# RWKV-7 layer of a hybrid decoder step: products, merges and gate of the late work in the dense products' PSUM banks

## The chip, the cores and the metric

The kernel runs on one core of one Trainium2 chip. The metric is the device time of one execution in microseconds; the kernel before takes 1889.89 us (median of three runs, 1886.84 to 1902.13). TensorE (PE) multiplies matrices into PSUM; VectorE (DVE), ScalarE (ACT) and GpSimd (POOL) read the results from there and work on them; SyncE (SP) issues DMA transfers, as ACT does for the weights.

## The reference

One inference step of a two-layer decoder in float32. Layer 0 mixes with a gated DeltaNet, layer 1 with RWKV-7; a causal ConvFFN follows each. 512 prompt tokens behind 16 meta tokens run as one sequence, 32 sample tokens (8 sequences of 4) from given states. Only the RWKV-7 mixer bears on the change:

```
def rwkv_step(S, xs):
    r_t, w_t, k_t, v_t, kk_t, a_t = xs
    sa = jnp.einsum('bhvk,bhk->bhv', S, kk_t)
    S = (S * w_t[:, :, None, :] - sa[..., None] * (kk_t * a_t)[:, :, None, :]
         + v_t[..., None] * k_t[:, :, None, :])
    y = jnp.einsum('bhvk,bhk->bhv', S, r_t)
    return S, y
...
    r = xr @ wr
    k = xk @ wk
    v = xv @ wv
...
    gate = jax.nn.sigmoid(xg @ g1) @ g2
...
    S, y = lax.scan(rwkv_step, S0.astype(F32), (tm(rh), tm(dh), tm(kh), tm(vh), tm(kk), tm(ah)))
...
    y = ((y - mu) * lax.rsqrt(var + GN_EPS)).reshape(B, L, D) * ln_w.astype(F32) + ln_b.astype(F32)
    bonus = jnp.sum(rh * kh * r_k.astype(F32), axis=-1, keepdims=True) * vh
    y = y + bonus.reshape(B, L, D)
    out = (y * gate.astype(F32)).astype(h.dtype) @ wo
```

The model width is 1024, with 16 heads of 64.

## The kernel before

All 560 tokens (32 sample, 16 meta, 512 prompt) lie in the free dimension, the 1024 channels as 8 blocks of 128 partitions. A dense product splits weights and input into a high and a low part and runs three matmuls for one (`dense_g`, L99, matmuls L114).

The function `rwkv` (from L1100) replaces the scan over tokens by chunks: chunk 0 of 48 tokens (16 of them meta), then eight of 64. The 16 heads go in two halves, G = 0 (the first heads) and G = 1 (the second heads). For a half and a chunk:

- `products` (L1412): 8 matmuls (L1420) into two PSUM banks give the chunk's 64 x 64 products of keys, receptances and decays; DVE masks them into SBUF (L1427, for chunk 0 L1424), POOL scales one block (L1433).
- `early` and `to_inverse` bring the triangular part of all chunks to DRAM; `inverse` (L1469) inverts the 32 x 32 triangles of chunks 1 to 8 at once on DVE (`tri_inplace`, L1071 and L1072), sends them to DRAM (UI) and loads them back into the products' tiles A (L1483, 16 DMAs on SP). `inverse0` does this for chunk 0.
- `merge` (L1505) makes 64 x 64 inverses out of 32 x 32 ones, for two chunks at a time (q = 0 to 3): a transpose on DVE (L1510), PE L1514, ACT L1515, PE L1519, ACT. Each merge starts the next.
- `rec` (L1639) is the serial recurrence of a half. After chunk 0 (L1665 to L1683), a chunk is a chain: PE L1695 and L1699, ACT L1700, PE L1704, DVE L1636, PE L1713, DVE L1715, then the next chunk; PE L1722 and DVE L1723 give its output. The second half's recurrence starts after the first's.
- `outnorm` (L1737) normalises two chunks' outputs (PE L1762), `samples` (L1779) runs the sample sequences (L1822 to L1845), `ktokens` and `vtokens` (L1540, L1562, L1584) rearrange keys and values, `gates` (L1596) computes the gate: 16 groups of four matmuls (L1618, L1619; 8 blocks, two halves of the tokens), each read by ACT (L1620) and DVE (L1621).

**PSUM.** It has eight banks. The pool `pd` (set up for the whole program) has two tiles of two banks, used by all dense products. The pool `pr` (L1108) has four single banks, handed out by `bank` (L487): recurrence, products, merges, norms, samples and gate share them in turn.

**Order.** The class `Weave` (L407) interleaves two kinds of generators with a modelled clock. `chains` are tried first, each with a time from which it may go on, as long as no more than two banks of `pr` are counted as held (`step`). Where none may, the next piece of the `slots` is issued. The slots of this layer stand in a row: dense k, r and v (8 blocks each), the products of the second heads (`products2`), the gate, and the output product of the first heads (osA, `out_half`). The output product of the second heads (osB) follows when all is done. A scheduler of the framework then sets the final order of each engine by its own estimates. Each engine takes its instructions in that order.

```
                if c[1] <= self.now and len(self.banks) <= 2:
```

```
        W.slots += [[None, products2()], [lambda: all(ktdone) and len(zdone) == KD and prod_done[1], gates()],
                    [lambda: normed[0] == 6 and bool(gated), out_half()]]
```

Of the kernel before, what the change touches and what calls it, by code (L numbers as in the profile page):

```python
# [8 lines left out]
F32 = mybir.dt.float32  # L9
# [8 lines left out]
P = 128  # L18
# [6 lines left out]
KD = 8  # L25
# [461 lines left out]
def bank_of(pg):  # L487
    def bank(shape):
        t = pg.tile([P, 512], F32, tag="pg", name="pg")
        n = int(np.prod(shape))  # L490
        v = t[:, :n]
        if len(shape) == 2:
            v = v.rearrange("p (a b) -> p a b", a=shape[0])
        elif len(shape) == 3:
            v = v.rearrange("p (a b c) -> p a b c", a=shape[0], b=shape[1])
        return v
    return bank


# [600 lines left out]
def rwkv(E, xp, norm, x_dram, sink):  # L1100


    nc, I, O = E.nc, E.I, E.O
    st = ExitStack()
    with st:
# [260 lines left out]
        def by_block(G, q):  # L1366
# [7 lines left out]
            nc.sync.dma_start(out=Dd[G], in_=t)  # L1374


        stA = ExitStack()
# [27 lines left out]
        def all_products(G):  # L1405
            for c in range(1, 9):
                A[G][c] = B["lo" if c < 5 else "hi"][G][:, (c - 1) % 4]
            for c in range(9):
                yield from products(G, c)
            prod_done[G] = True  # L1410

        def products(G, c):  # L1412

            o, n = col64(c)

            pa = [bank([4, 2, 64]) for hh in range(2)]
            for u in range(4):
# [48 lines left out]

        prod_done, merged = [False, False], [set(), set()]

        def inverse(G):  # L1469
            X, tmp = B["X"], B["tmp"]  # L1470
            nc.sync.dma_start(out=X, in_=LI[G].rearrange("j c h i t -> (j c h) i t"))
            for j in range(2):
                nc.sync.dma_start(out=D[64 * j:64 * j + 64], in_=Dd[G, 8:72, 32 * j:32 * j + 32])
            nc.vector.tensor_tensor(X, X, D.unsqueeze(1).to_broadcast([P, 32, 32]), op=ALU.mult)
            for _ in tri_inplace(E, X, tmp, P, 32):
                yield 0, E.d3, 0
            nc.sync.dma_start(out=UI[G].rearrange("j c h i t -> (j c h) i t"), in_=X)
            yield 0, E.invlag2, 0
            while not prod_done[G]:
                yield None  # L1480
            for c in range(8):
                for j in range(2):
                    nc.sync.dma_start(out=A[G][c + 1][64 + 32 * j:96 + 32 * j, :, 1, 32 * j:32 * j + 32],  # L1483
                                      in_=UI[G, j, c].rearrange("h i t -> i h t"))
            yield 0, 3.0, 0
            W.chain(merge(G, 0), first=True)

        def inverse0(G):
# [8 lines left out]
            yield 0, 8.0, 0  # L1497
            while not prod_done[G]:
                yield None
# [5 lines left out]
        def merge(G, q):  # L1505
# [5 lines left out]
            yield 0, 0.8, 0  # L1511
            py = bank([16, 32])
            for h in range(16):
                nc.tensor.matmul(py[r2, h, :], lhsT=Ac[r1, h, 1, 32:64], rhs=TY[r1, h, :], start=True, stop=True)  # L1514
            nc.scalar.activation(TY[r2], py[r2], AF.Copy)  # L1515
            yield 1.0, 1.0, 1
            pu = bank([16, 32])
            for h in range(16):
# [3 lines left out]
            merged[G].update((2 * q + 1, 2 * q + 2))  # L1522
            if q < 3:
                W.chain(merge(G, q + 1), first=True)

# [24 lines left out]
        v = H  # L1550
# [45 lines left out]
        def gates():  # L1596
# [4 lines left out]
            for b in range(2):  # L1601
# [13 lines left out]
                for m in range(KD):  # L1615
                    ps = bank([280])
                    for w, x in ((hi, gh), (hi, gl), (lo, gh)):
# [259 lines left out]
        def products2():  # L1877
            second_room()
            for w in all_products(1):
                yield w[0]  # L1880

        def seconds():
            for i, (r, f) in enumerate(((dn, ev_a), (up, ev_w))):
# [5 lines left out]
        W.slots += [[None, slot(ev_v(m))] for m in range(KD)]  # L1889
        W.slots += [[None, products2()], [lambda: all(ktdone) and len(zdone) == KD and prod_done[1], gates()],  # L1890
                    [lambda: normed[0] == 6 and bool(gated), out_half()]]
# [239 lines left out]
```

## Time and profile before

| | |
|---|---|
| median of three runs | 1889.89 us (1886.84 to 1902.13) |
| the profiled execution's own time | 1896.1 us |
| its span, first to last instruction | 1894.3 us |
| mean granted clock of TensorE | 0.951 |
| PE, DVE, ACT, POOL busy | 95%, 61%, 38%, 19% of the span |

The profile is of one execution. "Busy" of PE counts matmuls in flight, at whatever clock was granted to it, so that a stretch can be fully busy and still slow. In rows of the timeline the number in front is the start within the span, then the length; what stands in brackets is the idle time of the engine just before, and what ended it. The change touches the RWKV layer between about 1129 us, where the order of PE's instructions first differs, and 1429 us, where osB starts.

### The profile page before, as it was taken

The page shows a single profiled execution, that of the slowest core. Times are in us where ns is not written, and L with a number is a line of the kernel's source. Part 1 is how long each engine was busy: PE and PEld are TensorE (multiplying, and loading weights), DVE is VectorE, ACT ScalarE, POOL GpSimd, SP SyncE. Part 2 cuts the span into 40 slices and gives each one's busy share as a digit, 9 for nine tenths or more (in the row PEclk, how much of TensorE's full clock was granted, in tenths as well). Part 3 has the DMA queues.
Part 4 walks back from the last instruction along what each step waited for, and adds up shares of the span by engine and source line. Part 5 has one row for each costly group of instructions (what it writes and reads, how often), then busy time and mean ns, then how long its engine had stood idle before and what let it go on. Part 6 is the DMA issues. An engine that isn't in the chain of part 4 may idle for free.

```text
span 1894.3 us, 36496 instructions
## 1 busy us (share of the span) xinstructions
PE 1797.7 (95%) x14675; PEld 1716.2 (91%) x14675; DVE 1151.7 (61%) x2347; ACT 728.8 (38%) x1479; POOL 353.4 (19%) x608
## 2 busy tenths in 40 slices
PE   7999999999999999999998999799997999999997
PEld 7899998789999999998788998688786999999997
DVE  5698973875555553336588886866566455555223
ACT  4766434442232222222782245544323222222221
POOL 1442403621222220113011010021001111111010
PEclk9999998999999999999697999898898899999998
DMA  4233232333222223434111334342254222222332
GB/s 135 74 95 91 70 91 103 153 111 126 90 80 88 90 80 100 129 118 124 51 66 50 90 101 145 95 106 84 78 144 154 94 90 86 83 89 91 110 95 84
DMA packets 129825, 186.23 MB, mean 98 GB/s; under 512 B 63880, under 2 KB 78216, under 8 KB 129656
## 3 DMA queue, kind: packets, MB, share of 16 engines
q10 hardware_dynamic: 34448, 111.63, 17.8%
q1 hardware_dynamic: 95208, 72.27, 12.9%
q8 instruction: 116, 1.90, 0.4%
q14 instruction: 53, 0.43, 0.1%
HBM read 151.63 MB, written 32.22 MB: 97 GB/s over the span
## 4 chain that ended last, share of the span: by engine, by line
PE 77%; DVE 12%; ACT 3%; DMA 2%; issue 1%; SPq 0%; POOL 0%; ACTq 0%; DVEq 0%
PE pd L114 56%; PE pd L137 3%; PE pg L1420 1%; DVE lo L70 1%; DMA xo<-x 1%; PE pg L1699 1%; DVE it L473 1%; PE pg L1722 1%; PE pd L312 1%; PE pg L1269 1%; PE pg L1713 1%; PE pg L1822 1%; PE pg L1695 1%; PE pg L883 1%; PE pg L1704 1%
## 5 line engine op out<-in xcount | busy, mean ns | idle before, releaser
L114 PE MATMUL pd<-x,hi 128*128 128x280 f32 (+7 forms) x4768 | 843.1, 298 | 22.0 <-ACT hi L69 11.4
L114 PEld LDWEIGHTS pd<-x,hi 128*128 128x128 f32 (+1 forms) x4768 | 699.8, 193 | 30.0 <-ACT hi L69 12.0
L114 PE MATMUL pd<-x,lo 128*128 128x296 f32 (+5 forms) x2384 | 516.2, 297 | 4.7 <-DVE lo L70 4.7
L69 ACT ACTIVATE hi<-raw 128x1024 fp32r<-128x1024 f32 (+3 forms) x218 | 219.7, 1009 | 514.0 <-PE pd L114 475.3
L114 PEld LDWEIGHTS pd<-x,lo 128*128 128x128 f32 (+1 forms) x2384 | 384.9, 193 | 8.2 <-DVE lo L70 5.4
L70 DVE TENSOR_TENSOR lo<-raw,hi 128x1024 fp32r<-128x1024 f32 (+3 forms) x218 | 254.5, 1168 | 219.6 <-ACT hi L69 207.5
L217 POOL TENSOR_TENSOR s<-s,sq 128x560 f32<-128x560 f32 (+2 forms) x24 | 39.9, 1662 | 299.1 <-ACT sq L215 273.1
L347 DVE TENSOR_TENSOR gp<-pd,s 128x528 f32<-128x528 f32 (+1 forms) x44 | 30.8, 700 | 104.7 <-PE pd L114 104.6
L114 PE MATMUL pd<-hl,hi 128*128 128x280 f32 (+1 forms) x420 | 87.6, 290 | 0.0
L114 PE MATMUL pd<-hh,hi 128*128 128x280 f32 (+1 forms) x420 | 87.4, 289 | 0.0
L114 PE MATMUL pd<-hh,lo 128*128 128x280 f32 (+1 forms) x420 | 87.3, 289 | 0.0
L359 ACT ACTIVATE gs<-cv 128x528 f32<-128x528 f32 (+1 forms) x44 | 28.1, 639 | 147.4 <-DVE cv L357 147.3
L114 PE MATMUL pd<-hb,hi 128*128 128x280 f32 (+1 forms) x480 | 80.5, 290 | 0.0
L114 PEld LDWEIGHTS pd<-hb,hi 128*128 128x128 f32 x480 | 68.2, 188 | 0.0
L362 POOL TENSOR_TENSOR gs<-gs,s 128x560 f32<-128x560 f32 (+1 forms) x44 | 60.8, 1382 | 38.1 <-ACT gs L360 38.1
L365 DVE TENSOR_TENSOR h<-pd,gs 128x560 f32<-128x560 f32 (+1 forms) x44 | 32.1, 730 | 57.0 <-POOL gs L362 57.0
L114 PEld LDWEIGHTS pd<-hh,lo 128*128 128x128 f32 x420 | 66.4, 188 | 0.0
L114 PEld LDWEIGHTS pd<-hl,hi 128*128 128x128 f32 x420 | 66.2, 188 | 0.0
L114 PEld LDWEIGHTS pd<-hh,hi 128*128 128x128 f32 x420 | 66.1, 188 | 0.0
L351 POOL COPY fnew<-gp 128x2 f32<-128x2 f32 x44 | 8.1, 184 | 292.6 <-DVE gp L347 292.6
L137 PE MATMUL pd<-os,hi 128*128 128x280 f32 x256 | 52.4, 302 | 2.9 <-ACT os L182 2.4
L641 DVE SCALAR_TENSOR_TENSOR cv<-gp,pv,cv 128x584 f32<-128x584 f32 x48 | 42.2, 879 | 14.7 <-POOL cv L639 14.5
(569 smaller groups left out, 3013.0 us busy)
## 6 DMA issues: line engine op xcount, KB each, us to landing
raw<-w_up ACTq DMA_DIRECT2D x88, 512.0 KB
raw<-w_in ACTq DMA_DIRECT2D x32, 512.0 KB
raw<-w_down ACTq DMA_DIRECT2D x32, 512.0 KB
raw<-w_down ACTq DMA_DIRECT2D x16, 384.0 KB
kbd<-kst SPq DMA_DIRECT2D x18, 256.0 KB
KB<-kbd SPq DMA_DIRECT2D x18, 256.0 KB
xd<-xo SPq DMA_DIRECT2D x16, 280.0 KB
raw<-gdn_out ACTq DMA_DIRECT2D x8, 512.0 KB
```

The lines of the kernel that those rows point to most:

```text
L69: nc.scalar.activation(hi[:R, :kt, :M], raw[:R, :kt, :M], AF.Copy)
L70: lo_eng.tensor_tensor(lo[:R, :kt, :M], raw[:R, :kt, :M], hi[:R, :kt, :M].bitcast(F32), op=ALU.subtract)
L114: nc.tensor.matmul(ps[b][:M, :c1 - c0] if isinstance(ps, list) else ps[:M, b, :c1 - c0], lhsT=w[:, kk, :M], rhs=x[:, c0:c1], start=(k == 0 ...
L137: nc.tensor.matmul(ps[:, b, :c1 - c0], lhsT=a, rhs=x[:, c0:c1], start=(k == i == 0), stop=(k == len(xs) - 1 and i == 2))
L217: (eng or nc.gpsimd).tensor_tensor(self.acc[:, :self.w], self.acc[:, :self.w], sq, op=ALU.add)
L312: nc.tensor.matmul(ps[:, b, :c1 - c0], lhsT=a, rhs=x[:, c0:c1], start=(k == i == 0), stop=(k == len(xs) - 1 and i == 2))
L347: nc.vector.tensor_tensor(two(gp[:, m0:]), pm, two(s[:, mo:mo + ml]), op=ALU.mult)
L359: nc.scalar.activation(gs[:, mo:mo + ml], cv[:, m0 - 2:], AF.Silu)
L362: nc.gpsimd.tensor_tensor(gs, gs, s[:, :n_main], op=ALU.mult)
L365: nc.vector.tensor_tensor(two(h), ps[:, :, :hw], two(gs), op=ALU.mult)
L473: nc.vector.tensor_tensor(t.rearrange("p n j -> p j n"), U[:n, i:R, c0:], L[:n, i, i:R].unsqueeze(2).to_broadcast([n, m, k]), op=ALU.mult)
L641: nc.vector.scalar_tensor_tensor(cv, gp[:, i:i + 584], cw[i], cv, op0=ALU.mult, op1=ALU.add)
```

## The change

`late_bank` hands out halves of a tile of `pd`: two banks in a row from one tile, then a new tile. The second heads' products and merges and the gate take their banks there in place of `pr`. `prod_done` says chunk by chunk which products are made; chunk 0's inverse waits for chunk 0's only. `inverse` loads the inverses in four groups of two chunks, and one chain (`merges`) runs the four merges in a row, each no earlier than 2 units of the modelled clock after its group's loads. This holds for both halves; the bank changes for the second heads alone. The number of matmuls stays.

```diff
--- before.py
+++ after.py
@@ -486,15 +486,17 @@
 
 def bank_of(pg):
     def bank(shape):
-        t = pg.tile([P, 512], F32, tag="pg", name="pg")
...
+        return shaped(pg.tile([P, 512], F32, tag="pg", name="pg"), shape)
     return bank
+
+
+def shaped(t, shape):
+    v = t[:, :int(np.prod(shape))]
...
+    return v
@@ -1373,6 +1375,15 @@
+        spare = []
+
+        def late_bank(shape):
+
+            if not spare:
+                t = E.pd.tile([P, 2, 512], F32, tag="pd", name="pd")
+                spare.extend((t[:, 0], t[:, 1]))
+            return shaped(spare.pop(0), shape)
@@ -1407,13 +1418,13 @@
             for c in range(9):
                 yield from products(G, c)
-            prod_done[G] = True
+                prod_done[G].add(c)
 
         def products(G, c):
 
             o, n = col64(c)
 
-            pa = [bank([4, 2, 64]) for hh in range(2)]
+            pa = [(late_bank if G else bank)([4, 2, 64]) for hh in range(2)]
@@ -1464,7 +1475,7 @@
-        prod_done, merged = [False, False], [set(), set()]
+        prod_done, merged = [set(), set()], [set(), set()]
 
@@ -1476,14 +1487,26 @@
             nc.sync.dma_start(out=UI[G].rearrange("j c h i t -> (j c h) i t"), in_=X)
             yield 0, E.invlag2, 0
-            while not prod_done[G]:
-                yield None
-            for c in range(8):
-                for j in range(2):
-                    nc.sync.dma_start(out=A[G][c + 1][64 + 32 * j:96 + 32 * j, :, 1, 32 * j:32 * j + 32],
-                                      in_=UI[G, j, c].rearrange("h i t -> i h t"))
-            yield 0, 3.0, 0
-            W.chain(merge(G, 0), first=True)
+            for q in range(4):
+                cs = (2 * q, 2 * q + 1)
+                while len(prod_done[G]) < 9:
+                    yield None
+                for c in cs:
+                    for j in range(2):
+                        nc.sync.dma_start(out=A[G][c + 1][64 + 32 * j:96 + 32 * j, :, 1, 32 * j:32 * j + 32],
+                                          in_=UI[G, j, c].rearrange("h i t -> i h t"))
+                if q == 0:
+                    W.chain(merges(G), 3.0, first=True)
+                loaded[G].append(W.now)
+                yield 0, 0.5, 0
+
+        loaded = [[], []]
+
+        def merges(G):
+            for q in range(4):
+                while len(loaded[G]) <= q or W.now < loaded[G][q] + 2.0:
+                    yield None
+                yield from merge(G, q)
 
@@ -1495,7 +1518,7 @@
             yield 0, 8.0, 0
-            while not prod_done[G]:
+            while 0 not in prod_done[G]:
                 yield None
@@ -1509,19 +1532,17 @@
-            py = bank([16, 32])
+            py = (late_bank if G else bank)([16, 32])
...
-            pu = bank([16, 32])
+            pu = (late_bank if G else bank)([16, 32])
...
             merged[G].update((2 * q + 1, 2 * q + 2))
-            if q < 3:
-                W.chain(merge(G, q + 1), first=True)
@@ -1613,7 +1634,7 @@
                 for m in range(KD):
-                    ps = bank([280])
+                    ps = late_bank([280])
@@ -1887,7 +1908,7 @@
-        W.slots += [[None, products2()], [lambda: all(ktdone) and len(zdone) == KD and prod_done[1], gates()],
+        W.slots += [[None, products2()], [lambda: all(ktdone) and len(zdone) == KD and len(prod_done[1]) == 9, gates()],
```

The change moves instructions. In the order's rows pd and pg are the names of a tile of `pd` and of a bank of `pr`; line numbers are those of the kernel whose order it is, and x8 counts equal instructions in a row. First PE, at chunk 1 of the first heads' recurrence. Before (L1695, L1699, L1704, L1713 and L1722 are the recurrence's chunk, L1540 to L1584 key and value tokens):

```order
L1695 MATMUL pg<-KB,KR 128x128 x4
L1699 MATMUL pg<-KB,XX 64x64 x7
L1699 MATMUL pg<-KB,XX 128x64
L1540 MATMUL pg<-cm,ks 128x128 x4
L1584 MATMUL pg<-prod,brk 128x280 x2
L1704 MATMUL pg<-KB,XX 64x64 x8
L1562 MATMUL pg<-cm,H 128x128 x4
L1563 MATMUL pg<-cm,H 64x128
L1713 MATMUL pg<-KB 128x128 x4
L1722 MATMUL pg<-KB,XX 64x64 x8
```

After; L1716, L1720, L1725, L1734 and L1743 are the recurrence's chunk, L1431 the products of the second heads, L1561 and L1605 tokens:

```order
L1431 MATMUL pd<-KR,KB 128x128 x16
L1716 MATMUL pg<-KB,KR 128x128 x4
L1720 MATMUL pg<-KB,XX 64x64 x7
L1720 MATMUL pg<-KB,XX 128x64
L1561 MATMUL pg<-cm,ks 128x128 x4
L1605 MATMUL pg<-prod,brk 128x280 x2
L1431 MATMUL pd<-KR,KB 128x128 x11
L1725 MATMUL pg<-KB,XX 64x64 x8
L1431 MATMUL pd<-KR,KB 128x128 x13
L1734 MATMUL pg<-KB 128x128 x4
L1743 MATMUL pg<-KB,XX 64x64 x8
L1431 MATMUL pd<-KR,KB 128x128 x16
```

The products, which before begin in chunk 4 (one chunk's eight at a time), now stand in chunks 1 to 3, between the recurrence's steps; three chunks' of them are ahead of chunk 1.

Then DVE at the same place. Before; L1636 and L1715 are steps of the recurrence, L1071 and L1072 of the inversion, L1577 and L1579 of the value tokens, L399 to L404 a reciprocal root:

```order
L1577 TENSOR_TENSOR prod<-KR,KB 128x512
L1579 TENSOR_SCALAR brk<-rc,pv 128x128
L1072 TENSOR_REDUCE X<-tri 128x16
L402 TENSOR_TENSOR rst<-rsi,gv 16x8
L1636 TENSOR_TENSOR KB<-pg,nw 64x512
L1071 TENSOR_TENSOR tri<-X 128x49
L403 SCALAR_TENSOR_TENSOR rst<-rst,rsi 16x8
L1072 TENSOR_REDUCE X<-tri 128x7
L1074 MEMSET X 128x23
L404 SCALAR_TENSOR_TENSOR rsi<-rst,rsi 16x8
L1071 TENSOR_TENSOR tri<-X 128x384
L402 TENSOR_TENSOR rst<-rsi,gv 16x8
```

After; L1657 and L1736 are the recurrence's steps, L1073, L1074 and L1076 the inversion, L1438 the products' evacuations:

```order
L1438 TENSOR_TENSOR A<-pd,rc 128x4x128 x2
L1073 TENSOR_TENSOR tri<-X 128x9
L1772 TENSOR_REDUCE gv<-KB 16x8
L1657 TENSOR_TENSOR KB<-pg,nw 64x512
L1074 TENSOR_REDUCE X<-tri 128x3
L1076 MEMSET X 128x21
L1438 TENSOR_TENSOR A<-pd,rc 128x4x128 x2
L1773 TENSOR_SCALAR gv<-gv 16x8
L1073 TENSOR_TENSOR tri<-X 128x374
L1438 TENSOR_TENSOR A<-pd,rc 128x4x128 x2
L399 TENSOR_SCALAR rsi<-gv 16x8
L1074 TENSOR_REDUCE X<-tri 128x17
```

Evacuations of the products now stand between inversion and recurrence, where there were none of them in these rows before.

Last PE at the gate. Before, with the last gate groups (L1618, L1619) ahead of the second recurrence's first step (L1665); L1519 and L1514 are merges, L1821, L1822 and L1841 samples:

```order
L1618 MATMUL pg<-gs,hi 128x280 x2
L1618 MATMUL pg<-gs,lo 128x280
L1619 MATMUL pg<-gs,hi 128x280
L1519 MATMUL pg<-A,TY 32x32 x16
L1822 MATMUL pg<-A 128x128 x7
L1821 MATMUL pg<-A 32x64 x2
L1822 MATMUL pg<-A 128x128
L1665 MATMUL pg<-KB,A 16x64 x8
L1841 MATMUL pg<-XX 128x512
L1514 MATMUL pg<-TY,A 32x32 x16
```

After; L1639 and L1640 are the gate, L1537 a merge, L1783 a norm, the rest chunks 6 and 7 of the first recurrence:

```order
L1743 MATMUL pg<-KB,A 64x64 x7
L1639 MATMUL pd<-gs,hi 128x280 x2
L1639 MATMUL pd<-gs,lo 128x280
L1640 MATMUL pd<-gs,hi 128x280
L1537 MATMUL pd<-TY,A 32x32 x12
L1716 MATMUL pg<-KB,KR 128x128 x4
L1720 MATMUL pg<-KB,A 64x64 x7
L1720 MATMUL pg<-KB,A 128x64
L1850 MATMUL pg<-XX,A_11995 32x64 x2
L1537 MATMUL pd<-TY,A 32x32 x4
L1639 MATMUL pd<-gs,hi 128x280 x2
L1639 MATMUL pd<-gs,lo 128x280
```

The gate's groups, all between chunk 8 and L1665 before, now begin in chunk 6 of the first recurrence: 6 of 16 stand ahead of its chunk 8, 3 between this and the start of the second recurrence (L1686), and 7 behind it.

More of the change, by code (lines that the diff above doesn't have):

```diff
@@ L488, in bank @@
     def bank(shape):
-        t = pg.tile([P, 512], F32, tag="pg", name="pg")
[L490 to L496, printed above, removed]
-    return bank
+        return shaped(pg.tile([P, 512], F32, tag="pg", name="pg"), shape)
+    return bank
+def shaped(t, shape):
+    v = t[:, :int(np.prod(shape))]
+    if len(shape) == 2:
+        v = v.rearrange("p (a b) -> p a b", a=shape[0])
+    elif len(shape) == 3:
+        v = v.rearrange("p (a b c) -> p a b c", a=shape[0], b=shape[1])
+    return v
 def gdn(E, xp, norm, x_dram, sink):
```

## The prediction

> **What bounds the kernel now.** I read the page's busy shares first, then the chain that ended last, then the windows of the stretch that the change touches, cut at events of the serial recurrence.
>
> ```profile
> PE 1797.7 (95%) x14675; PEld 1716.2 (91%) x14675; DVE 1151.7 (61%) x2347; ACT 728.8 (38%) x1479; POOL 353.4 (19%) x608
> ...
> PE 77%; DVE 12%; ACT 3%; DMA 2%; issue 1%; SPq 0%; POOL 0%; ACTq 0%; DVEq 0%
> ```
>
> TensorE (PE) is busy for 95% of the span and carries 77% of the chain. A change that leaves the matmuls as they are can win back only time in which PE is idle, or busy at a lowered clock. The windows below give both. Their columns are the window, its length, busy time of PE, of its weight loads, of DVE, ACT and POOL, the granted clock, DMA share and GB/s. 1183.93 is the start of chunk 1 of the first heads' recurrence (its L1695), 1231.26 that of chunk 5, 1262.33 that of chunk 8; 1301.39 is the start of the second heads' recurrence (L1665), 1312.79 its chunk 1, 1402.61 its chunk 8, 1429.21 the first output product of its heads (osB).
>
> ```profile
> 1183.93:1231.26 47.33, 36.01 (x314) 31.11 (x314) 38.09 (x116) 26.29 (x82) 2.81 (x7) 0.86 0.32 95
> 1231.26:1262.33 31.07, 30.07 (x315) 26.55 (x313) 21.12 (x49) 14.76 (x48) 6.11 (x14) 1.00 0.35 89
> 1262.33:1301.39 39.06, 36.67 (x329) 31.18 (x329) 29.37 (x74) 20.92 (x60) 7.82 (x20) 0.91 0.40 109
> 1301.39:1312.79 11.40, 11.40 (x183) 9.69 (x183) 4.85 (x10) 3.92 (x10) 2.92 (x4) 1.00 0.47 139
> 1312.79:1402.61 89.82, 85.95 (x778) 74.38 (x778) 55.21 (x142) 30.75 (x82) 5.50 (x12) 0.87 0.31 92
> 1402.61:1429.21 26.60, 17.67 (x152) 15.69 (x150) 20.34 (x53) 5.16 (x11) 1.27 (x3) 0.90 0.44 122
> ```
>
> Length less PE busy is 11.3 + 1.0 + 2.4 + 0 + 3.9 + 8.9 = 27.5 us idle. Busy time times one less the clock is 5.0 + 0 + 3.3 + 0 + 11.2 + 1.8 = 21.3 us, the estimate of what the lowered clock costs. So the whole stretch of 245.3 us holds at most some 49 us to win. The clock's part has a clear place:
>
> ```profile
> 1318.95 2.05 PE L1713 MATMUL pg<-KB 128*128 128x128 f32 x8 [0.83 <-DVE KB L1636]
> 1320.93 1.27 PE L1514 MATMUL pg<-TY,A 32*32 32x32 f32 x20
> ...
> 1320.00:1325.00 5.00, 5.00 (x54) 4.48 (x53) 1.43 (x3) 1.87 (x5) 0.00 (x0) 0.50 0.17 52
> 1325.00:1330.00 5.00, 5.00 (x40) 4.54 (x41) 0.68 (x1) 0.60 (x1) 0.00 (x0) 0.50 0.08 26
> 1330.00:1335.00 5.00, 5.00 (x39) 3.31 (x37) 0.69 (x1) 0.59 (x1) 1.04 (x1) 0.50 0.02 3
> ```
>
> For 15 us PE has no gap and yet runs at half clock, so 7.5 us are lost there. The 0.83 us gap and small matmuls of a merge (32x32) stand at its start.
>
> **The products, +12.7 us.** The second heads' chunk products (8 matmuls, 2 evacuations a chunk) took their PSUM banks from the pool of four that the recurrence uses, and so went one chunk at a time into its chunks 4 to 8. Now they take halves of the dense pool's two tiles, and the order puts three chunks' matmuls ahead of chunk 1 and the other six inside chunks 1 to 3. All full-size evacuations then queue on DVE there, among the triangular inversion:
>
> ```profile
> L1072 DVE TENSOR_REDUCE X<-tri 128x19 f32<-128x380 f32 (+23 forms) x24 | 10.1, 421 | 0.6
> L1071 DVE TENSOR_TENSOR tri<-X 128x378 f32<-128x378 f32 (+20 forms) x23 | 9.7, 423 | 0.5
> ...
> L1424 DVE TENSOR_TENSOR A<-pg,rc 128x192 f32<-128x192 f32 x4 | 1.2, 350 | 0.0
> ...
> L1427 DVE TENSOR_TENSOR A<-pg,rc 128x512 f32<-128x512 f32 x16 | 10.4, 682 | 4.3 <-PE pg L1420 4.2
> ```
>
> The first three are of the window 1183.93 to 1231.26, the last of the whole stretch. DVE, at 38.09 of 47.33 us (0.805), is already what the recurrence waits for:
>
> ```profile
> 1191.84 0.68 DVE L1577 TENSOR_TENSOR prod<-KR,KB 128x512 f32<-128x512 f32 x1
> ...
> 1192.63 0.53 DVE L1072 TENSOR_REDUCE X<-tri 128x16 f32<-128x368 f32 x1
> ...
> 1193.38 0.69 DVE L1636 TENSOR_TENSOR KB<-pg,nw 64x512 f32<-64x512 f32 x1
> ...
> 1194.13 2.08 PE L1713 MATMUL pg<-KB 128*128 128x128 f32 x8 [2.94 <-DVE KB L1636]
> ```
>
> L1636 stood behind other DVE work, and PE waited 2.94 us. With the products DVE's work between chunk 1 and chunk 5 is 38.09 − 1.2 (chunk 0's evacuations, now earlier) + 10.4 = 47.3 us. Packed without a gap this is 47.3, at today's 0.805 it is 58.8; with the 1.2 us ahead of chunk 1 the stretch becomes 48.5 to 60.0, where it was 47.33. I take 60.0, since the recurrence still waits in every chunk and an evacuation now stands between two inversion steps: +12.7, with +1.2 as the other end. The POOL operation of each chunk (L1433) goes with it. PE is not the limit: 36.01 plus six chunks less one at 1.53 us (4.6 us for three, the row below) is some 44.
>
> **Chunks 5 to 8, −0.5.** They lose the products and gain 6 of the gate's 16 groups of four matmuls.
>
> ```profile
> L1420 PE MATMUL pg<-KR,KB 64*128 64x128 f32 x80 | 7.8, 285 | 0.0
> ...
> L1618 PE MATMUL pg<-gs,hi 128*128 128x280 f32 x32 | 9.1, 366 | 0.4 <-ACT gs L1609 0.4
> L1618 PE MATMUL pg<-gs,lo 128*128 128x280 f32 x16 | 5.2, 328 | 0.0
> L1619 PE MATMUL pg<-gs,hi 96*128 96x280 f32 x16 | 5.1, 328 | 0.0
> L1420 PE MATMUL pg<-KR,KB 64*128 64x128 f32 x48 | 4.6, 285 | 0.0
> ```
>
> (The first row is of 1231.26 to 1262.33, the others of 1262.33 to 1301.39.) −7.8 + 6/16 × 19.4 = −0.5.
>
> **From chunk 8 to the second recurrence, −23.6.** All 16 gate groups, 9.1 + 5.2 + 5.1 = 19.4 us, stood here. In the new order 6 are earlier, 3 stay and 7 come after the second recurrence has begun: −13/16 × 19.4 = −15.8, and −4.6 for the products. Of this window's 5.7 us of idle and slow time (2.4 + 3.3) I let the share of the removed busy time go, 20.4/36.67, −3.2. Without that it is −20.4. Cover: the 7 late groups lie among the second recurrence's waits, where output products of the first heads (osA) lie today. Those are pushed behind it, the tail's term.
>
> **The second recurrence, +1.1 − 5.** By the new order the work from L1665 to chunk 1 rises from 11.5 to some 12.5 us: +1.1. From chunk 1 to chunk 8 gates replace an equal time of osA products. The full-array gates now stand where PE ran 15 us at half clock; I give back two thirds of 7.5, −5. Ends: 0 (the clock falls anyway) and −11.2 (no slow time in that window).
>
> The merges' new bank and the grouped loads cost or win little: the merge waited for loads 0.7 us in all, and the 16 loads, now before chunk 8's inputs on SP's queue, hold that queue 16 × 0.46 = 7.4 us, which is less than a chunk.
>
> ```profile
> L1510 DVE STREAM_TRANSPOSE TY<-A 32x512 f32<-32x512 f32 x6 | 4.2, 702 | 2.5 <-PE pg L1514 1.7 <-DMA A<-UI 0.7
> ...
> 1237.67 0.92 SPq L1483 DMA_DIRECT2D A<-UI  x2
> ```
>
> What would queue behind them are the K loads of chunk 8, the second gate input and, behind those, the samples' loads. Waiting there is covered by the six gate groups.
>
> **The tail, +5.4.**
>
> ```profile
> 1425.95 1.09 PE L1762 MATMUL pg<-cm,KB 128*128 128x128 f32 x4 [6.76 <-DVE rsi L399]
> ...
> 1429.21 0.83 PE L114 MATMUL pd<-osB,hi 128*128 128x274 f32 x2 [2.17 <-ACT osB L182]
> ...
> L114 PE MATMUL pd<-osA,hi 128*128 128x274 f32 x45 | 7.7, 290 | 0.0
> L114 PE MATMUL pd<-osA,lo 128*128 128x274 f32 x24 | 5.9, 314 | 0.0
> ```
>
> After chunk 8 13.6 us of osA products are left now. By the new order some 7 us more are left (8.5 us of late gates, less what fits into gaps). They stand ahead of the last norm's matmuls, so 1.6 of the 6.76 + 2.17 us of waits is filled and the rest stays, because the products' own evacuations queue on DVE before the norm: +7 − 1.6 = +5.4. If they fill the waits wholly, the end is 0.
>
> **Sum:** +12.7 − 0.5 − 23.6 + 1.1 − 5 + 5.4 = −9.9 us. The profiled execution took 1896.1 us (its span is 1894.3), 6.2 above the median 1889.89. So about 1886 for a like execution and **1880** for the median. With every term at its better end it is +1.2 − 0.5 − 23.6 + 1.1 − 11.2 + 0 = −33; at its worse, +12.7 − 0.5 − 20.4 + 1.1 + 0 + 5.4 = −1.7.
>
> **Rivals.**
>
> *PE fills up* (0.20). DVE packs, so the first term is +1.2, and the clock stays full in the second recurrence, −11.2: with the tail's +5.4 the sum is −27.6, **1862**. For it: PE has 11.3 us idle in chunks 1 to 5 that the products can fill, and the clock was 1.00 in the two windows with almost no idle. Against: DVE would have to run without a gap. The Trainium skill speaks for this rival in two places. Its page "Perfetto Trace Analysis", section "Matmul Optimizations", asks to use all eight PSUM banks, which the change does. Its page "TensorE: Matmul & The Clock Gate", section "The HAM clock gate (the "warmup" mystery)", has half clock only after an idle window of about 3.4 us, and full clock after such a time of sustained work; by that rule no slow time would be left. The rows of 1320 to 1335 disagree: 15 us of unbroken work stayed at 0.50 after a gap of 0.83 us. So I leave the chance low.
>
> *The time only changes place* (0.19). PE's work is the same; if waits and slow clock follow the recurrence instead of the gates, the 49 us stay. The sum is 0 ± 4, **1890**. For it: the recurrence's links (L1636, L1715) are untouched, and the worse ends above sum to −1.7. Against: between chunk 8 and 1301.39 PE does work that no link needs.
>
> *Two tiles are too few* (0.14, slower). PE takes its instructions in order; when both dense tiles await evacuation, the recurrence's matmuls stand behind the next product or gate. Price: each of 16 evacuations with one inversion pair ahead of it, (0.68 + 0.42 + 0.42) × 16 = 24.3; 16 gate evacuations at 0.497, 7.8 of DVE on the path; half clock over 15 us as seen above, 7.5.
>
> ```profile
> L1621 DVE SCALAR_TENSOR_TENSOR H<-H,pv,pg 128x280 f32<-128x280 f32 x16 | 7.8, 497 | 2.5 <-ACT KB L1620 2.4
> ```
>
> With −0.5 − 23.6 + 1.1 + 5.4 from above the sum is +22, **1912**. It decides once the products' stretch is longer by over 17.6 us than now (47.33 to 65). Against: the tiles are split into banks, and three chunks go ahead of chunk 1.
>
> **Chances and range.** The forecast has 0.47, the others 0.20, 0.19 and 0.14. 1% is 18.9 us, about what a measurement of this kernel can tell from no change (its runs lie between 1886.84 and 1902.13). Faster by over that, below 1871: nearly all of the first rival and the forecast's lower part (0.10), 0.30. Slower, above 1908.8: most of the last rival, 0.11. The rest is 0.59. The range 1861 to 1899 leaves out some 0.12 above and 0.08 below. The forecast's own range is 1866 to 1888.
>
> **What would show it.** Chunk 1 to chunk 5 of the first recurrence near 60 us with DVE above 0.78 busy (below 52: PE fills up; above 65: too few tiles, with waits before the products' matmuls that DVE's L1438 ends). Chunk 8 to the second recurrence near 15.5. Granted clock in the second recurrence's chunks above 0.90. Chunk 8 to osB near 32, with osA products behind it for some 20 us. If chunks 5 to 8 take well over 31 us, gates cost more there than their busy time, and the sum is wrong in a place that I priced at nothing.

## The result

The changed kernel takes 1874.97 us (median of 20 runs, 1867.74 to 1891.98) against 1888.26 us for the kernel before (20 runs, 1882.91 to 1902.13). The medians lie 13.3 us apart; the ratio is 0.9927, 95% interval 0.991 to 0.9943. The forecast had 9.9 us less and 1880 us for the time. All ratios are of runs in the fast state, which leaves out one run of e3 (2657.2 us) and one among those of the kernel before that were timed beside e1 to e4 (2143.39 us).

First the windows of the changed kernel's profile (execution 1873.39 us, span 1871.6), cut at the same events as those of before: chunk 1, chunk 5 and chunk 8 of the first recurrence, the start of the second, its chunk 1, its chunk 8, the first osB product. Columns as before.

```profile
1175.32:1231.37 56.05, 42.34 (x397) 36.69 (x395) 45.64 (x128) 25.38 (x81) 7.68 (x15) 0.82 0.26 76
1231.37:1265.31 33.94, 31.09 (x327) 26.84 (x325) 18.47 (x47) 18.95 (x57) 3.08 (x9) 0.95 0.42 105
1265.31:1280.92 15.61, 14.88 (x147) 11.73 (x144) 10.69 (x30) 9.80 (x31) 3.69 (x10) 1.00 0.43 124
1280.92:1293.75 12.83, 12.83 (x177) 11.29 (x177) 6.21 (x19) 6.55 (x19) 3.83 (x10) 1.00 0.43 113
1293.75:1377.62 83.87, 81.15 (x782) 71.03 (x782) 62.30 (x158) 35.90 (x96) 6.92 (x12) 0.92 0.33 96
1377.62:1408.71 31.09, 24.76 (x202) 21.91 (x201) 21.83 (x57) 6.42 (x14) 2.32 (x4) 0.94 0.61 172
```

The lengths that were 47.33, 31.07, 39.06, 11.40, 89.82 and 26.60 us are 56.05, 33.94, 15.61, 12.83, 83.87 and 31.09. The stretch falls from 245.3 to 233.4 us. The two profiled spans differ by 22.7 us, more than the medians do. Some 10 us of that lie ahead of the change: the same four matmuls (L1584 before, L1605 after), which stand ahead of any difference in the order, started at 1125.51 and at 1115.70 us. To separate such differences both kernels were profiled once more.

```
label            kernel
e8_before_again  the kernel before, unchanged
e9_after_again   the changed kernel, unchanged
```

> The kernel before once more, for a second profile. If the granted clock's low stretches are fixed by the order of instructions: chunk 1 to chunk 5 again 47 us at 0.86, the second recurrence's chunks again 90 us at 0.87, 900 to 940 us again at about 0.6. If they fall by chance: lengths that differ by 4 to 10 us in some of these stretches with the idle time about the same.

> The changed kernel once more, for a second profile. Theory: what differed between the two profiles of before (c. 10 us ahead of the change, at 900 to 940 us) is chance, while the stretches of the recurrences follow from the order: chunk 1 to chunk 5 again 54 to 58 us with about 11 us of waits of the norm's matmul, chunk 8 to the second recurrence again 15 to 16, the second recurrence's chunks 82 to 86 at a clock of 0.90 to 0.95. Rival (the clock's part is chance everywhere): one of these differs by over 4 us.

The windows of before's second profile (1884.52 us, span 1882.7):

```profile
1172.19:1220.59 48.40, 38.22 (x315) 33.04 (x315) 38.19 (x116) 26.40 (x83) 2.83 (x7) 0.82 0.32 94
1220.59:1251.56 30.97, 30.06 (x314) 26.53 (x313) 21.15 (x49) 14.46 (x47) 6.12 (x14) 1.00 0.34 88
1251.56:1291.74 40.18, 37.81 (x329) 32.33 (x329) 29.37 (x74) 21.16 (x60) 7.84 (x20) 0.87 0.39 104
1291.74:1303.14 11.40, 11.40 (x184) 9.69 (x183) 4.86 (x10) 3.92 (x10) 2.93 (x4) 1.00 0.51 147
1303.14:1395.04 91.90, 88.06 (x778) 76.15 (x778) 55.21 (x142) 30.77 (x82) 5.51 (x12) 0.83 0.30 91
1395.04:1421.63 26.59, 17.66 (x151) 15.68 (x149) 20.33 (x53) 5.15 (x11) 1.27 (x3) 0.86 0.43 119
```

And those of the changed kernel's second profile (1870.39 us, span 1868.6):

```profile
1175.33:1231.62 56.29, 42.58 (x397) 36.87 (x395) 45.65 (x127) 25.47 (x81) 7.70 (x15) 0.82 0.26 76
1231.62:1263.99 32.37, 29.51 (x326) 25.45 (x324) 18.47 (x47) 18.84 (x57) 3.08 (x9) 1.00 0.42 107
1263.99:1280.17 16.18, 15.46 (x147) 11.73 (x144) 10.70 (x30) 10.38 (x32) 3.69 (x10) 0.96 0.41 124
1280.17:1297.16 16.99, 16.99 (x177) 15.08 (x177) 6.17 (x19) 5.86 (x17) 3.83 (x10) 0.73 0.33 92
1297.16:1378.16 81.00, 78.28 (x781) 68.39 (x781) 62.38 (x158) 35.90 (x96) 6.92 (x12) 0.96 0.33 97
1378.16:1409.26 31.10, 24.76 (x202) 21.91 (x201) 21.85 (x56) 6.42 (x14) 2.32 (x4) 0.94 0.59 171
```

The sums are 249.4 us for before and 233.9 for the changed kernel, so from kernel to kernel the mean difference is 233.7 − 247.4 = −13.7 us. A single window moves by up to 4.2 us from one profile to the other (12.83 and 16.99), where the clock's slow time falls elsewhere; the rival of e9's expectation is right in that, by the letter. Of e8's expectation the first half holds for the two recurrences (48.40 and 91.90 us), the second for 900 to 940 us. The largest difference between two profiles of one kernel lies ahead of the change. Before's two profiles between 900 and 940 us, the first one above, the second below:

```profile
900.00:920.00 20.00, 18.02 (x82) 14.34 (x80) 14.57 (x22) 13.94 (x29) 0.11 (x1) 0.72 0.27 94
920.00:940.00 20.00, 20.00 (x57) 14.40 (x57) 8.44 (x11) 13.16 (x26) 1.21 (x3) 0.50 0.08 27
```

```profile
900.00:920.00 20.00, 18.02 (x83) 13.79 (x81) 13.95 (x21) 15.30 (x35) 0.11 (x1) 0.83 0.22 79
920.00:940.00 20.00, 17.57 (x108) 14.05 (x108) 14.28 (x17) 19.17 (x32) 4.26 (x9) 0.99 0.08 27
```

In the second window one execution ran 57 matmuls at a clock of 0.50, the other 108 at 0.99, and the same program reached chunk 1 at 1183.93 and at 1172.19 us. Such differences, like the 10 us above, are no effect of the change.

### The profile page after: what moved, and what is told of

The parts are those of the page before. It is cut to its first block, busy times and chain, and to the rows that moved or that the text cites. A ratio compares the mean times of both kernels' runs of the same rounds, so it can differ in the third digit from the quotient of the medians.

```text
span 1871.6 us, 36493 instructions
## 1 busy us (share of the span) xinstructions
PE 1773.6 (95%) x14675; PEld 1697.4 (91%) x14675; DVE 1151.3 (62%) x2347; ACT 728.8 (39%) x1481; POOL 356.7 (19%) x608
## 4 chain that ended last, share of the span: by engine, by line
PE 78%; DVE 11%; ACT 3%; DMA 2%; issue 1%; SPq 0%; ACTq 0%; DVEq 0%
PE pd L114 57%; PE pd L137 3%; DMA xo<-x 1%; DVE lo L70 1%; PE pg L1843 1%; PE pg L1720 1%; DVE it L473 1%; PE pd L312 1%; PE pg L1743 1%; PE pg L1431 1%; PE pg L1725 1%; PE pg L1716 1%; PE pg L885 1%; PE pg L1734 1%; DVE cv L643 1%
## 5 line engine op out<-in xcount | busy, mean ns | idle before, releaser
L114 PE MATMUL pd<-x,hi 128*128 128x280 f32 (+7 forms) x4768 | 835.6, 296 | 22.0 <-ACT hi L69 11.2
```

Of the source, the lines that this page charges most:

```text
L114: nc.tensor.matmul(ps[b][:M, :c1 - c0] if isinstance(ps, list) else ps[:M, b, :c1 - c0], lhsT=w[:, kk, :M], rhs=x[:, c0:c1], start=(k == 0 ...
```

## The experiments

### Which part of the change it is

Two kinds of edits were made together: three uses got other banks, and the conditions under which inverses and merges go on were altered. Four kernels take them apart. e1 moves all three banks and keeps loads, merges and conditions of before (against the changed kernel):

```diff
-            for q in range(4):
-                cs = (2 * q, 2 * q + 1)
...
+            while len(prod_done[G]) < 9:
+                yield None
+            for c in range(8):
...
+            yield 0, 3.0, 0
+            W.chain(merge(G, 0), first=True)
...
-            while 0 not in prod_done[G]:
+            while len(prod_done[G]) < 9:
...
+            if q < 3:
+                W.chain(merge(G, q + 1), first=True)
```

> The three uses take their banks from the dense pool, but loads, merges and the conditions of the inverses are those of before. Theory of the prediction (the gate's banks shorten the stretch from chunk 8 to the second recurrence): most of the 23 us come back, that stretch falls from 39 to 20 us or less, and the ratio to before is 0.993 or less. Rival (the start of the second recurrence is set by when chunk 0's inverse may go on, not by the banks): by the order 6 gate groups still stand in that stretch with all merges, it stays at 30 to 34 us, chunks 1 to 5 of the first recurrence still pay for the products (55 to 57 us against 47), and the ratio is 0.998 to 1.005.

e2 does the opposite: no bank is moved, the grouped loads, the chain of merges and chunk 0's own condition stay.

```diff
-            pa = [(late_bank if G else bank)([4, 2, 64]) for hh in range(2)]
+            pa = [bank([4, 2, 64]) for hh in range(2)]
...
-            py = (late_bank if G else bank)([16, 32])
+            py = bank([16, 32])
...
-            pu = (late_bank if G else bank)([16, 32])
+            pu = bank([16, 32])
...
-                    ps = late_bank([280])
+                    ps = bank([280])
```

> No bank is moved; only the grouped loads, the one chain of merges and chunk 0's own condition are those of the changed kernel. Theory of the prediction: the banks are what frees PE, so this is worth little, ratio 0.998 to 1.004, with chunk 8 to the second recurrence at 33 us or more. Rival (the conditions set it): chunks 1 to 5 stay at 47 us, chunk 8 to the second recurrence falls to 16 to 19 us, its start to chunk 1 grows from 11.4 to 17, and the ratio is 0.992 to 0.997, about as good as the whole change.

e3 takes only the first of these four edits (the products go back); e11 is the same kernel once more. e4 is the kernel before with one line changed:

```diff
-            while not prod_done[G]:
+            while 0 not in prod_done[G]:
                 yield None
             for j in range(3):
```

(with `prod_done` kept by chunk.)

> The changed kernel with the second heads' products back in the recurrence's pool; gate and merges stay in the dense pool. Theory (the early products cost 8 to 9 us on DVE and bring nothing by themselves): chunks 1 to 5 return from 56 to 47 us, chunks 5 to 8 take 32 to 34, chunk 8 to the second recurrence 16 to 18, and the ratio to before is 0.990 to 0.994, as good as the whole change or better. Rival (early products are what lets everything behind them start early): chunk 8 to the second recurrence is over 25 us and the ratio is 0.997 or more.

> e3 once more: products in the recurrence's pool, all else as changed. If the order brings the half clock: chunk 8 to the second recurrence is again 24 to 25 us, fully busy at 0.67, and the ratio is again 0.998 to 1.003. If it was chance: that stretch takes 16 to 18 us at 1.00, and the ratio comes to 0.993 to 0.997.

> The kernel before with one condition changed: chunk 0's inverse of a half waits for chunk 0's products alone. Theory of the prediction: nothing, 0.998 to 1.003. Rival (this condition holds the second recurrence back): chunk 8 to the second recurrence falls from 39 to 16 to 20 us, its start to chunk 1 grows to 19 since 11 gate groups stand there, and about 18 us more output products are left behind its chunk 8; the ratio is 0.993 to 1.000.

| kernel | ratio to before | 95% interval | runs |
|---|---|---|---|
| changed kernel | 0.9927 | 0.991 to 0.9943 | 20 |
| e1, banks alone | 0.9988 | 0.9968 to 1.0008 | 10 |
| e2, no bank moved | 0.9941 | 0.9913 to 0.9968 | 7 |
| e3, products back | 1.0008 | 0.9981 to 1.0035 | 9 |
| e11, the same again | 0.9954 | 0.9918 to 0.9991 | 10 |
| e4, one condition | 0.9984 | 0.9964 to 1.0004 | 10 |

The banks alone show no gain; the conditions without any bank show one, by the two ratios four fifths of the whole (0.59% of 0.73%, with an interval from 0.32% to 0.87%). The intervals of e1 and e2 touch at 0.9968. The windows show what moves. e1, chunk 1 to 5 and chunk 8 to the second recurrence:

```profile
1180.99:1236.03 55.04, 44.05 (x380) 37.83 (x378) 44.00 (x125) 26.81 (x84) 7.16 (x14) 0.81 0.26 75
...
1267.51:1304.34 36.83, 32.04 (x339) 26.91 (x337) 21.20 (x54) 18.26 (x53) 5.75 (x17) 0.81 0.38 112
```

e2, the first four windows:

```profile
1171.43:1223.93 52.50, 42.80 (x315) 36.76 (x315) 38.63 (x119) 26.72 (x84) 2.81 (x7) 0.74 0.30 88
1223.93:1254.86 30.93, 30.70 (x319) 27.21 (x317) 21.33 (x49) 15.48 (x50) 6.11 (x14) 1.00 0.34 92
1254.86:1272.23 17.37, 17.37 (x161) 14.35 (x161) 11.50 (x29) 8.34 (x29) 5.50 (x13) 1.00 0.46 125
1272.23:1291.29 19.06, 17.98 (x233) 15.78 (x232) 14.02 (x37) 10.95 (x31) 3.83 (x10) 1.00 0.36 92
```

With the banks alone, 36.83 us still pass between chunk 8 and the second recurrence, though 10 of the 16 gate groups have left that stretch in its order. Without any bank moved it is 17.37 us. (e2's chunks 1 to 5 were expected at 47 us. They took 52.50, with less idle time than before, 9.7 us, but at a clock of 0.74.) The second recurrence may start once chunk 0's inverse of its heads is there, and that waited for all nine chunks' products. That condition, not the gate's bank, held it. By the old order the gate, next in the slots, was issued whole in the meantime.

The early start is not yet a gain, as e4 shows (chunk 8 to the second recurrence, to its chunk 1, to its chunk 8, to osB):

```profile
1257.57:1274.96 17.39, 17.39 (x161) 14.37 (x161) 11.86 (x30) 8.69 (x29) 5.50 (x13) 1.00 0.48 128
1274.96:1301.74 26.78, 24.65 (x253) 21.90 (x252) 17.39 (x43) 13.44 (x38) 3.82 (x10) 0.81 0.28 74
1301.74:1387.20 85.46, 80.53 (x737) 67.92 (x735) 54.08 (x143) 30.08 (x81) 5.50 (x12) 0.78 0.24 72
1387.20:1426.35 39.15, 36.11 (x292) 33.20 (x290) 24.50 (x59) 7.96 (x16) 2.47 (x2) 1.00 0.51 151
```

The stretch is as short as e2's, but 26.78 us follow before chunk 1, the clock is 0.78 over the second recurrence, and 36 us of work are left behind it. The clock's estimate (busy time times one less the clock) over the six windows is 36.3 us in e4's one profile, 22.2 in e2's, 21.3 and 29.2 in before's two, 17.2 and 17.5 in the changed kernel's. Idle time is 20.6, 20.3, 27.5 and 26.2, 26.3 and 26.4 us. So e2 and e4 both have some 6 to 7 us less idle than before, and e4 loses them to the clock in its one profile (1889.56 us, 3.4 above its median). Why this execution ran at a lower clock was not tried. Nor were the grouped loads and the one chain of merges, which e2 has beyond e4, run by themselves. So it is shown which condition shortens this stretch, but not which of the conditions brings e2's gain over e4.

e3 has the new conditions and all new banks but the products', and yet was no better than before in one set of runs and half a per cent better in the other. It has all of e2's conditions, so these do not bring the gain in every order. Chunk 8 to the second recurrence, e3 and then e11:

```profile
1266.79:1291.61 24.82, 24.82 (x156) 20.52 (x156) 10.32 (x20) 8.41 (x27) 5.02 (x13) 0.67 0.30 89
```

```profile
1252.82:1274.91 22.09, 22.09 (x156) 18.07 (x156) 10.33 (x20) 8.42 (x27) 5.04 (x13) 0.77 0.34 99
```

e2 runs 161 matmuls there in 17.37 us at a clock of 1.00; e3 and e11 run 156 in 22 to 25 us, without one gap in PE, at 0.67 and 0.77. Busy time times the clock is about the same in all three, some 17 us, so the work is much the same and the clock makes the difference. Their sums over the six windows agree (245.1 and 245.3). So the slow time is there in both profiles of this order. That the order is its cause is not shown by two profiles: the changed kernel's 12.83 and 16.99 us above, at 1.00 and 0.73, are one order too. The reason stays open: by the order the stretch holds much the same work in both kernels (three chunks' products each, two gate groups against e2's three). Open too is why one kernel's two ratios lie as far apart as 1.0008 and 0.9954, on two chips; their intervals share only 0.9981 to 0.9991, and the single runs of e11 lie between 1868.53 and 1891.86 us. A difference of less than half a per cent between two kernels here is not to be trusted from one set of runs; that between e1 and e2 is 0.47%.

### What lengthens the first chunks

In chunks 1 to 5 the changed kernel is 56 us long where before is 47 and 48. Of the 8.3 us more (means of two profiles) 5.3 are busy time of PE, since six chunks' products now stand there (L1431, 7.5 us), and 3.0 are idle time. The largest idle time by PE group in 1175.32 to 1231.37, and some rows on ACT and PE at chunk 2:

```profile
L1783 PE MATMUL pg<-cm,KB 16*128 16x16 f32 (+1 forms) x8 | 2.1, 353 | 11.0 <-ACT KB L1779 11.0
```

```profile
1198.71 2.02 ACT L1779 ACTIVATE KB<-KB,gr 16x64 f32<-16x64 f32 x8 [3.96 <-DVE gr L404]
```

```profile
1199.35 0.28 PE L1783 MATMUL pg<-cm,KB 16*128 16x16 f32 x1 [5.24 <-ACT KB L1779]
1199.57 1.97 PE L1725 MATMUL pg<-KB,XX 64*64 64x64 f32 x16
```

11.0 of the 13.7 us of idle are one kind of wait: the norm's transposes (L1783) stand in PE's order ahead of the recurrence's next step (L1725), and wait for ACT, which waits for the root's last step (L404) on DVE, behind inversion and evacuations. In before's window 1183.93 to 1231.26 the same wait was 4.6 us, and the wait for L1636, the step that the prediction looked at, was 4.7:

```profile
L1762 PE MATMUL pg<-cm,KB 16*128 16x16 f32 (+1 forms) x8 | 1.6, 274 | 4.6 <-ACT KB L1758 4.6
L1713 PE MATMUL pg<-KB 128*128 128x128 f32 x32 | 7.1, 395 | 4.7 <-DVE KB L1636 4.7
```

In the changed kernel the latter (L1657 there) is down to 0.3 us:

```profile
L1734 PE MATMUL pg<-KB 128*128 128x128 f32 x32 | 6.2, 356 | 0.3 <-DVE KB L1657 0.3
```

e5 puts the first heads' norm later, e6 takes half of the evacuations off DVE, e7 doubles them:

```diff
-            yield 0, 6.0, 0
+            yield 0, (6.0 if G else 15.0), 0
```

> The changed kernel with the first heads' norm matmuls put off by 9 more units of the modelled clock, so that they stand later in PE's order; all else of it is unchanged in kind. Theory A (what lengthens chunks 1 to 5 is the norm's matmul, which stands ahead of the recurrence's steps in PE's order and waits 11 us for DVE's reciprocal root): chunk 1 to chunk 5 falls from 56 to 46 to 50 us, the norm's waits go, and the ratio to before is 0.984 to 0.990. Theory B (the prediction's: DVE itself is the pace there): DVE's work is the same, chunk 1 to chunk 5 stays at 54 to 58, the waits pass to the recurrence's own DVE steps, ratio 0.991 to 0.995.

```diff
+                    if G and hh:
+                        nc.scalar.activation(A[G][c][:, hh::2], pa[hh], AF.Copy)
+                        nc.gpsimd.tensor_tensor(A[G][c][:, hh::2], A[G][c][:, hh::2], m_, op=ALU.mult)
+                    else:
+                        nc.vector.tensor_tensor(A[G][c][:, hh::2], pa[hh], m_, op=ALU.mult)
```

> The changed kernel, with half of the second heads' product evacuations (8 of 16 in chunks 1 to 8) taken off DVE: ACT copies them, POOL masks them in SBUF. Theory B (DVE sets the pace of chunks 1 to 5): 5.2 us less DVE work there, chunk 1 to chunk 5 falls from 56 to about 51, ratio to before 0.988 to 0.991. Theory A (the norm's place sets it): the root's chain gets through DVE only a little earlier, 54 to 56 us, ratio 0.991 to 0.995.

```diff
+                    for _ in range(2 if G else 1):
+                        nc.vector.tensor_tensor(A[G][c][:, hh::2], pa[hh], m_, op=ALU.mult)
```

> The changed kernel with each of the second heads' 16 full-size product evacuations done twice on DVE: 10.9 us more DVE work in the first recurrence's early chunks. Theory B: chunk 1 to chunk 5 grows by 9 to 11, to 65 to 67 us, ratio 0.997 to 1.000. If DVE has slack there: 58 us or less, ratio 0.992 to 0.995.

Ratios to before: e5 0.9914 (0.988 to 0.9948, 4 runs), e6 0.994 (0.9913 to 0.9967, 6 runs), e7 0.9983 (0.9957 to 1.001, 10 runs). Chunk 1 to chunk 5 of e5, and its last window:

```profile
1176.04:1224.68 48.64, 39.38 (x400) 33.79 (x398) 44.66 (x126) 24.68 (x79) 7.78 (x15) 0.96 0.28 83
...
1390.25:1409.65 19.40, 9.15 (x73) 7.67 (x73) 12.07 (x34) 3.49 (x10) 0.22 (x2) 0.73 0.12 35
```

Of e6 and e7, chunk 1 to chunk 5:

```profile
1177.27:1233.62 56.35, 44.16 (x396) 37.72 (x394) 46.01 (x120) 29.93 (x89) 18.59 (x23) 0.82 0.26 77
```

```profile
1176.37:1238.99 62.62, 46.63 (x396) 40.04 (x394) 55.27 (x144) 25.85 (x81) 8.31 (x15) 0.75 0.23 69
```

e5 settles the place: with nearly the same work on DVE (44.66 us, now 92% of the window) the stretch falls by 7.4 us to 48.64. DVE could have gone at that pace; the norm's place in PE's queue was what didn't let it. Of the 7.41 us 4.45 are idle time and 2.96 busy time: about as many matmuls (400 and 397) ran at a clock of 0.96 in place of 0.82, and why is not shown.

e7 shows that DVE's work still counts, but by another way. Its evacuations hold up the products' next matmuls (L1431), which stand ahead of the recurrence's steps, while the norm's wait (L1784) is shorter than the changed kernel's:

```profile
L1431 PE MATMUL pd<-KR,KB 64*128 64x128 f32 x98 | 9.1, 333 | 7.6 <-DVE A L1440 7.6
...
L1784 PE MATMUL pg<-cm,KB 16*128 16x16 f32 (+1 forms) x8 | 2.5, 358 | 5.8 <-ACT KB L1780 5.8
```

9.6 us more on DVE made the stretch 6.6 us longer, 2.3 of them idle and 4.3 busy time at a lower clock (0.75). That lies between its two expectations (65 to 67 us, or 58 and less). e6 did not lighten DVE at all, 46.01 us busy, for a reason told in the last section, so it doesn't tell the two theories apart.

e5's 7.4 us were given back, so that its ratio stays above the 0.984 to 0.990 of its theory A: its six windows sum to 233.6 us, as the changed kernel's 233.4. In its order the osA products start in chunk 4 of the second recurrence and are used up by its end, and the last window has 10.3 us idle (19.40 − 9.15). e10 puts the norm off less, so that osA stays for the tail; e12 does the same to e2, without any moved bank:

```diff
-            yield 0, 6.0, 0
+            yield 0, (6.0 if G else 12.0), 0
```

> The changed kernel with the first heads' norm put off by 6 units in place of 9 (e5). By the order some 32 us of work are left behind the second recurrence's chunk 8, most of it output products, where e5 left 7. Theory (e5's early gain went into the tail, where PE had nothing left): chunk 1 to 5 at 48 to 50 us as in e5, chunk 8 to osB 35 to 38 with under 5 us idle, ratio to before 0.985 to 0.989. Rival (the tail's waits are bound by the norm's chain whatever stands there): chunk 8 to osB is over 40 us, ratio 0.991 to 0.995.

> e2 (no bank moved; grouped loads, chain of merges, chunk 0's own condition) with the norm put off as in e10. If the banks bring something of their own: ratio 0.992 to 0.996, as e2 or a little better, and over 2 us behind e10. If the conditions and the norm's place are all: chunk 1 to 5 at 44 to 50 us, ratio 0.985 to 0.990, as e10.

e10 comes to 0.993 (0.9904 to 0.9956, 10 runs), e12 to 0.9894 (0.9824 to 0.9964, 4 runs, median 1866.66 us). Start of the second recurrence to its chunk 1, and the last window, of e10:

```profile
1276.39:1310.45 34.06, 32.51 (x354) 27.11 (x354) 17.03 (x39) 14.53 (x36) 5.00 (x9) 0.65 0.33 98
...
1377.83:1417.17 39.34, 35.27 (x265) 33.21 (x265) 29.37 (x77) 10.52 (x21) 1.05 (x1) 0.93 0.52 157
```

Chunk 1 to 5 of e12:

```profile
1171.26:1213.83 42.57, 37.11 (x326) 32.11 (x327) 36.72 (x113) 22.97 (x72) 3.54 (x8) 0.88 0.33 93
```

e10's tail does fill (4.1 us idle), but its 32.51 us of busy time at 0.65 cost 11.4 us by the clock's estimate in another window. Its ratio is that of the changed kernel, not the 0.985 to 0.989 that was expected. e12 has the lowest median of all the kernels, with no bank moved; its interval holds the changed kernel's ratio and e10's, and its six windows sum to 238.3 us in one profile, so it isn't shown to be better. It is shown to be faster than before, by 0.3% at least, and so is e2, so the moved banks aren't needed for a gain.

## Why the prediction was right, and where it was wrong

The time was right, and so was the largest term. Four of the other terms are off by 2.4 to 3.4 us, two each way, and their errors nearly cancel, which is luck. Means of two profiles each, after less before:

| term | forecast | measured |
|---|---|---|
| ahead of chunk 1 (1.2 of the products' 12.7) | +1.2 | +1.2 |
| products: chunk 1 to 5 | +11.5 | +8.3 |
| chunk 5 to 8 | −0.5 | +2.1 |
| chunk 8 to the second recurrence | −23.6 | −23.7 |
| its start to chunk 1 | +1.1 | +3.5 |
| its chunks 1 to 8 | −5 | −8.4 |
| tail | +5.4 | +4.5 |
| sum | −9.9 | −12.5 |

(The first row is of the first profiles alone, from the same L1584 matmuls to chunk 1, 58.42 and 59.62 us.) The medians lie 13.3 us apart.

- *Products.* DVE was 0.81 busy, as assumed. That DVE's share sets the pace was wrong: the step "since the recurrence still waits in every chunk" took the wrong wait. 11.0 of 13.7 us of idle stand ahead of the norm's transposes, and with these moved DVE ran at 92% (e5). In this term the prediction spoke of L1636 only, and that wait fell to 0.3 us. Most of the growth is busy time of PE, 5.3 of 8.3 us, which the prediction set aside ("PE is not the limit").
- *Chunks 5 to 8.* The sign was wrong. In 1231.37 to 1265.31 PE is idle for 2.9 us, before for 1.0; the gate's matmuls wait 1.9 us there for DVE (L1633), a wait that the prediction had priced at nothing and named as a place to look.
- *Chunk 8 to the second recurrence.* The size was right to 0.1 us, the cause was not seen. The step reads "In the new order 6 are earlier, 3 stay and 7 come after", and does not say what moves them; the expectations of e1 and e2 put that down to the banks, as this prediction's theory. The prediction says that "The merges' new bank and the grouped loads cost or win little" and does not price chunk 0's condition at all. e1 has the gate's banks without it and keeps 36.83 us; e2 and e4 have it without the banks and come to 17.37 and 17.39. The sum was right because it was read from the order of the whole change, which holds both.
- *The second recurrence.* The clock rose from 0.87 and 0.83 to 0.92 and 0.96, and the term was 3.4 us too small, within its own ends (0 to −11.2). That it rose because full-array gates stand among the small matmuls is not shown. From 1310 to 1320 us the changed kernel's first profile has PE busy without a gap at 0.50, with two gate groups in it. In its second, two matmuls of the gate took 0.53 us, and in the next group 0.83, where the clock was 0.65 (1315 to 1320 us):

```profile
1314.97 0.53 PE L1639 MATMUL pd<-gs,hi 128*128 128x280 f32 x2
...
1318.05 0.83 PE L1639 MATMUL pd<-gs,hi 128*128 128x280 f32 x2
```

e7 has five gate groups in the second recurrence's chunks 1 to 8 and ran this stretch at 0.79; e10 has none there and ran it at 0.97. From the start to chunk 1 the term was 2.4 us too small, mostly because the second profile had a clock of 0.73 there.

- *Tail.* 31.1 us in both profiles, forecast 32. The last norm's wait is 4.16 us in place of 6.76.

```profile
1405.43 1.11 PE L1783 MATMUL pg<-cm,KB 128*128 128x128 f32 x4 [4.16 <-DVE KB L1776]
```

- *The rivals.* "Two tiles are too few" did not come: the waits ahead of the products' matmuls are 0.8 us in chunks 1 to 5. With twice the evacuations they are 7.6 (e7), so the mechanism is there.

```profile
L1431 PE MATMUL pd<-KR,KB 64*128 64x128 f32 x98 | 7.5, 284 | 0.8 <-DVE A L1438 0.4 <-DVE tri L1073 0.3
```

"The time only changes place" is what e1 and e4 are: work moved, and no gain is shown (0.9988 and 0.9984, both intervals reach 1). "PE fills up" did not come either. Of the 13.7 us by which the stretch is shorter, idle time gives 0.5; the clock's estimate falls by 7.9 (21.3 and 29.2 to 17.2 and 17.5), and the other 5 or so are mostly work that now stands ahead of chunk 1 (three chunks' products, 4.6 us before). Since before's own two estimates lie 8 us apart, the clock's share is rough. The prediction read the moved banks as what the Trainium skill asks for, to use all eight PSUM banks (page "Perfetto Trace Analysis", section "Matmul Optimizations"); by themselves they came to 0.9988.

## What to carry to other kernels

When a change moves resources and conditions together, the order of the whole gives its sum but not its cause: look for the one condition that the critical step waits on, and build the halves apart before crediting the resource. In an in-order queue, look at what stands ahead of the serial chain's next step; a side result (here a norm) that waits for another engine stops the chain however short it is. And count slow clock as a term of its own beside idle: here it was up to 36 of 254 us (e4's one profile) and took back what less idle had given.

## What the runs showed of the hardware

**Half clock in unbroken work.** PE ran 20 us without a gap at 0.50 (920 to 940 us in before's first profile, above), and 22 to 25 us at 0.67 and 0.77 in e3 and e11. The matmuls of the first are mostly of the full array (128x128 weights), and the same program did it in one profile and not in the next. The 15 us at 0.50 that the prediction shows, 1320 to 1335 us, came again in before's second profile, 1310 to 1325 us. By the Trainium skill's page "TensorE: Matmul & The Clock Gate", section "The HAM clock gate (the "warmup" mystery)", half clock follows an idle window and full clock a few us of sustained work; the traces here disagree with the second half of that, as long as busy means what the profile counts.

**POOL holds DVE up.** In e6 POOL masks 128x512 tiles in SBUF. A DVE step on 16x8 numbers, both inputs in SBUF, that falls into such an operation lasts until it ends; first DVE, then POOL:

```profile
1198.23 1.12 DVE L403 SCALAR_TENSOR_TENSOR rst<-rst,rsi 16x8 f32<-16x8 f32 x1
```

```profile
1198.06 1.27 POOL L1441 TENSOR_TENSOR A<-A,rc 128x512 f32<-128x512 f32 x1 [3.79 <-DVE rst L402]
```

In the changed kernel such steps take 0.16 us, as most of L403's do in e6. DVE's busy time did not fall although 5.5 us of evacuations left it (46.01 against 45.64 us). The Trainium skill says this on its page "SBUF — State Buffer", section "SBUF: two separate sides": one port pair is shared and held for a whole instruction. The trace agrees: L403 ends at 1199.35, POOL's operation at 1199.33.
